# A Trainium2 decoder layer: a thirteenth sevenfold pair in the first half's down passes, four more weight sums made ahead, and the closing scalings cut into 512 and 256 columns

## The chip, the cores and the metric

The kernel runs on one core of one Trainium2 chip. The metric is the device time of one execution in microseconds, taken as the median of several runs of the same program.

## What is computed

One decoder layer over 256 tokens of width 2048 in float32: a normalised input goes through one wide projection, a recurrent branch and a windowed attention branch run side by side, both are gated, merged and projected by `w_out`, and a squared-ReLU MLP of width 8192 follows. The change touches the MLP's down projection, and its preparation is spread over the rest of the layer:

```
x = x + rmsnorm(mix @ w_out, norm_mix_post)
h = rmsnorm(x, norm_mlp_pre)
u = square(relu(h @ w_mlp_up))          # 256 x 8192
x = x + rmsnorm(u @ w_mlp_down, norm_mlp_post)
```

## The kernel before

**Matmuls in two parts.** Every weight chunk and every activation is split into a high part that TensorE takes exactly and a low part, the rest. A product is three matmuls: high by high, high by low, low by high. So each weight half (a tile of 128 by 1024) needs one cast on ScalarE (`whi`, L176) and one subtraction on VectorE (`wlo`, L181). `Stream` (L62) does this for all weights in one order: SyncE loads halves into raw buffers (`wraw`, `xraw`, `more`), the two engines split them into six `whi` and six `wlo` buffers, TensorE uses them. A load waits until the subtraction has read the raw buffer that it goes into; a cast waits until TensorE is done with the `whi` buffer that it goes into.

**The order of the stages.** Projections and attention come first, then the recurrent branch with `attn_proj` (L943 to L959, m = 0 to 3), the merge, the product with `w_out` in two passes (`o_pass`, L1024, called at L1058 and L1076), and the MLP. The MLP runs in two halves f of 4096 channels. Each half makes its 16 activation pairs (the up products, `a_pair`), and then runs two down passes (`down`, L1275), n = 0 and 1, of 1024 output columns each, over the same 16 pairs.

**Sevenfold pairs.** Most of the 16 pairs of a down pass are multiplied by a Strassen-Winograd scheme: seven block products in place of eight, each of three matmuls of 512 columns, so 21 matmuls in place of 24. `KINDS` (L41) gives each pair of each pass a digit. "1" is a plain pair (24 matmuls, two weight halves). The others are sevenfold; they need sums of weight blocks, and the digit says where these are made. With "3" the stream itself makes three of them on VectorE (L149 to L151) just before use. With "2" two blocks come ready from memory and one difference is made in the stream (L147). With "4" everything comes ready. A "1" or "3" loads 1 MB, a "2" 1.25 MB, a "4" 1.75 MB. A sevenfold pair splits three halves and a further 128 by 512 tile (`t2hi`, `t2lo`).

**Sums ahead.** What "2" and "4" read is made earlier by `sums_ahead` (L405), one generator for each such chunk: GpSimd's queue loads the 1 MB chunk into the tile `early` (L410), VectorE adds in place (L414, L416 for a "4" only, L419, L420), and GpSimd's queue writes 0.5 or 1 MB to memory (L422). `in_turn(n, every, wait)` starts n of them, one for each `every` halves of weights that the stream hands out, after `wait` halves. A generator takes one step for each half handed out (`begin`, L204): the load at its first step, L414 and L416 at its fifth, L419 and L420 at its sixth, the write at its seventh. Two rules place them:

```
not_before(nc.gpsimd.dma_start(w, chunks[c]))     # L410: waits for the latest wlo made so far
with tc.issue_after(ws.latest_low.ins):           # L413: VectorE does it after the latest wlo
```

So in the usual course four `wlo` lie between a load and the first sum that reads it.

**The end of the `w_out` product.** In the second pass the last four weight halves are held back (`held`, L1076): the stream hands them out one right behind the other, with no matmul between. TensorE then finishes the first 128 tokens (`last_step`, L1080), then the others. Meanwhile VectorE multiplies the results by a gain (`gained`, L1054), sums the squares, and scales (`norm`, L1089; `scaled`, L1087); TensorE transposes the scaled rows (`turned`, L1103) for the MLP. All of these are pinned in program order on their engines.

**The end of the kernel.** In the last down pass, `finish` (L1448) scales a token block's 2048 outputs and adds the residual with one instruction of 1024 columns and two of 512 (L1484), each followed by a store (L1485).

Of the kernel before, what the change touches and what calls it, by code (L numbers as in the profile page):

```python
# [18 lines left out]
F32 = mybir.dt.float32  # L19
F32R = mybir.dt.float32r  # L20
# [5 lines left out]
P = 128  # L26
# [11 lines left out]

PAIRS = 16

KINDS = ("1242423142424211", "1242423142422411"), ("4242424242421111", "4242424242441111")  # L41
SEVENS = [[p for p in range(PAIRS) if k[0][p] != "1"] for k in KINDS]


# [197 lines left out]
def layer(tc, x, few, kx_first, kx_rest, pos_row, gains, w_q, w_xy, w_rg, w_g, w_rp, w_ap, w_out,  # L242
          w_up, w_dn, out):
    nc = tc.nc
# [35 lines left out]
    for f in range(2):  # L280
        chunks += [w_up[32 * f + i] for i in range(32)]
        for n in range(2):
            sums.update((len(chunks) + i, KINDS[f][n][i]) for i in SEVENS[f])
            plain_down.update(len(chunks) + i for i in range(PAIRS) if i not in SEVENS[f])
            chunks += [w_dn[(2 * f + n) * PAIRS + i] for i in range(PAIRS)]

    def unit(name, dt=F32R):
        return big.tile([P, 4, 2, S], dt, tag="U8", name=name)

    def flat(t):  # L290
        return t.rearrange("p a b c -> p (a b c)")

    ws = Stream(nc, wpool, chunks, sums)

    def units(name):
        return [unit(f"{name}{i}") for i in range(4)]
# [128 lines left out]
    def in_turn(n, every, wait=0):  # L425

        for i in range(wait):
            yield
        left, active, at = [sums_ahead(to_sum.pop(0)) for i in range(min(n, len(to_sum)))], [], 0
        while left or active:  # L430
            if left and at % every == 0:
                active.append(left.pop(0))
            at += 1
            active = [g for g in active if next(g, active) is not active]
            yield
# [11 lines left out]
    def quarter(q):  # L447
        return slice(q * 512, q * 512 + 512)
# [49 lines left out]
    pin = ws.pin = tc.keep_in_program_order  # L498
# [303 lines left out]
    def wide(t):  # L802
        return t.rearrange("p (f t) -> p f t", f=2)
# [126 lines left out]
    def recur(m):  # L930
        room = flat(unit("xct", F32)).rearrange("p (n c) -> p n c", c=512)
        for i in range(2):
            conv(2 * m + i, room[:, i, :])
        for i in range(2):
            gelu(2 * m + i, room[:, 2 + i, :])
# [7 lines left out]
    for m in range(4):  # L943
        if m == 2:
            more = flat(unit("more", F32))
            for i in range(2):
                ws.add(ws.raws, more[:, i * 1024 : i * 1024 + 1024])
        recur(m)
        if m == 0:
            pump(99)  # L950
            ctx_ps.close()
            psg = ctx1.enter_context(tc.tile_pool(name="psg", bufs=2, space=bass.MemoryType.PSUM))
            pairs.append(ctx1.enter_context(tc.tile_pool(name="psa2", bufs=1, space=bass.MemoryType.PSUM)))
        if m < 2:
            ws.side.append(in_turn(2, 6))
            for i in range(2):
                attn_proj(2 * m + i)
        if m < 3:
            gates(m)  # L959
# [50 lines left out]
    x1 = po.tile([P, TB, D], F32, name="x1")  # L1010
# [33 lines left out]

    r1 = []
    late = []
    ws.side.append(in_turn(4, 6, 2))
    h2T = units("h2T")

    def square(tb, q, b):  # L1050
# [135 lines left out]
    for tb in range(TB):  # L1186
        for i in range(2):
            q = 2 + i
# [50 lines left out]

    o_v = out.rearrange("(t p) d -> t p d", p=P)  # L1240

    def evacuate(f, p, u, dst):
        nc.scalar.activation(u, u, AF.Relu)
        nc.scalar.activation(u, u, AF.Square, scale=SHRINK)
        if p not in SEVENS[f]:
            nc.scalar.copy(dst[:, :, 0, :], wide(u))
            nc.vector.tensor_tensor(dst[:, :, 1, :], wide(u), dst[:, :, 0, :].bitcast(F32), ALU.subtract)
            return

        e = u2("e")  # L1250
        u4, e4 = [t.rearrange("p (a b) -> p a b", a=4) for t in (u, e)]
        nc.vector.tensor_tensor(e4[:, 0:2], u[:, 0:P].unsqueeze(1).to_broadcast([P, 2, P]), u4[:, 1:3], ALU.subtract)
        nc.vector.tensor_tensor(e4[:, 2], e4[:, 1], u4[:, 1], ALU.subtract)
        nc.vector.tensor_tensor(e4[:, 3], e4[:, 2], u4[:, 3], ALU.add)
        for to, of in zip(dst, (u4[:, 1:4], e4)):
            nc.scalar.copy(to[:, 0], of)
            nc.vector.tensor_tensor(to[:, 1], of, to[:, 0].bitcast(F32), ALU.subtract)
# [98 lines left out]
    for f in range(2):  # L1356
        uT = {}
        rooms = []
        if f:
            ws.side.append(in_turn(10, 5))  # L1360
        full = []
        for p in range(PAIRS):
            u = u2("u")
            if f == 0 and p == 1:
                ws.side.append(in_turn(7, 4, 8))
            if f == 0 and p in (4, 6):
                not_before(nc.gpsimd.dma_start(h2T_away[p // 2 - 2], h2T[p // 2].bitcast(F32)))
            if f == 0 and p < 2:
                up_pair(p, wide(u))
            else:  # L1370
                a_pair(h2T, wide(u), PRIO if p == PAIRS - 1 else 0)
            full.append((p, u))
            if f == 0 and p == R2_AT:
                pump(99)
                ctx3.close()
                pc = ctx2.enter_context(tc.tile_pool(name="pc", bufs=1))
                ws.small = pc
                ws.add(ws.raws, pc.tile([P, 1024], F32, name="xraw"))
                ws.t2_raws, ws.t2_highs, ws.t2_lows = [[Slot() for i in range(n)] for n in (3, 2, 2)]
            if f == 1 or p >= R2_AT:  # L1380
                for q, u in full:
                    if q % 2 == 0:
                        rooms.append(unit(f"uT{f}{q}"))
                    room = rooms[-1][:, 2 * (q % 2) : 2 * (q % 2) + 2]
                    if q in SEVENS[f]:
                        three = pc.tile([P, 2, 3, P], F32R, tag="three", bufs=max(map(len, SEVENS)), name=f"three{f}{q}")
                        uT[q] = three, flat(room).rearrange("p (a b c) -> p a b c", a=2, b=4)
                    else:
                        uT[q] = room
                    evacuate(f, q, u, uT[q])  # L1390
                full.clear()
# [21 lines left out]
        accs, x1 = [], []  # L1413

        def acc(tb, q):
            return accs[q // 2][:, tb, quarter(q % 2)]
# [31 lines left out]
        def finish(name, b, t, at, w, fold=lambda: None):  # L1448
            tb, i = name
            q = 2 * n + i  # L1450
            a = acc(tb, q)
            if n == 0:
                nc.vector.tensor_tensor(a, b, t, ALU.add)
                nc.scalar.activation(t, a, AF.Square, scale=r2_squared[tb], accum_out=sq3[:, tb, q : q + 1])
                return
            p = slice(at, at + w)
            k = q + (at > 0)
            pin(nc.vector.tensor_tensor(a[:, p], b[:, 0:w], t[:, p], ALU.add))
            if not spare:
                spare.append(flat(unit("spare", F32)))  # L1460
            pin(nc.scalar.activation(spare[0][:, p], a[:, p], AF.Square, scale=r2_squared[tb],
                                     accum_out=sq3[:, tb, k : k + 1]))
            pin(nc.vector.scalar_tensor_tensor(t[:, p], a[:, p], r2_squared[tb],
                                               g3[0][:, q * 512 + at : q * 512 + at + w], ALU.mult, ALU.mult))
            last[tb, i] = t
            fold()
            r, to = [st[:, 12 + 2 * tb + k : 13 + 2 * tb + k] for k in range(2)]
            if at + w < 512:
                pin(nc.vector.tensor_reduce(r, sq3[:, tb, 0:4], AX.X, ALU.add))
                pin(nc.vector.tensor_scalar(before, r, 1.0 / D, EPS, ALU.mult, ALU.add))  # L1470
                return
            if i:
                if tb:
                    pin(nc.scalar.activation(to, sq3[:, tb, 4:5], AF.Sqrt, bias=before, scale=1.0 / D))
                else:
                    pin(nc.vector.tensor_reduce(r, sq3[:, tb, 0:4], AX.X, ALU.add))
                    pin(nc.scalar.activation(to, r, AF.Sqrt, bias=eps, scale=1.0 / D))
                pin(nc.vector.reciprocal(r, to))
                scaled[tb] = r
            if i:  # L1480
                for k in (0, 2, 3):
                    c = quarter(k) if k else slice(0, 1024)
                    g = last[tb, k - 2] if k else accs[0][:, tb]
                    pin(nc.vector.scalar_tensor_tensor(x1[tb][:, c], g, scaled[tb], x1[tb][:, c], ALU.mult, ALU.add))  # L1484
                    pin((nc.scalar if k == 2 else nc.sync).dma_start(o_v[tb][:, c], x1[tb][:, c]))  # L1485

        n = 0
        g3, spare, before = [], [], st[:, 29:30]
# [2 lines left out]
        last, scaled = {}, {}  # L1491
# [82 lines left out]
```

## Time and profile before

| | |
|---|---|
| median of 3 runs | 1481.5 us (1481.31 to 1482.2) |
| the profiled execution | 1481.78 us |
| its span, first to last instruction | 1479.9 us |
| TensorE busy / VectorE / ScalarE | 99% / 80% / 60% |
| mean granted TensorE clock | 0.999 |
| sums ahead (1 MB loads by GpSimd's queue) | 46 |
| moved by DMA | 411 MB, 278 GB/s over the span |

The span is 1.9 us shorter than the profiled execution's own time. PE is TensorE, DVE is VectorE, ACT is ScalarE, POOL is GpSimd, SP is SyncE. Matmuls are pipelined: each lasts 389 ns, but they start closer together than that, so the distance between starts counts. Times in views are from the span's start.

### The profile page before, as it was taken

To read this page: it belongs to the slowest core of one execution; us is meant where nothing else is said; L and a number is where in the kernel's file an instruction comes from. 1 tells how busy PE (TensorE), PEld (TensorE's weight loads), DVE (VectorE), ACT (ScalarE), POOL (GpSimd) and SP (SyncE) were. 2 spreads that over 40 slices of the span, in tenths; PEclk is the share of its full clock that TensorE was granted. 3 is DMA by queue.
4 is the path that set the end of the run, shared out by engine and by line. 5 is a ranking of instruction groups with operands and counts; after the bars stand their busy time and mean duration, and the time that the engine had idled before them with its cause. 6 is when DMAs were issued, how large, how long until landed. Compare 5 with 4: busy or idle time off the path is not lost.

```text
span 1479.9 us, 20692 instructions
## 1 busy us (share of the span) xinstructions
PE 1470.3 (99%) x7520; PEld 1247.2 (84%) x7520; DVE 1182.8 (80%) x1546; ACT 884.4 (60%) x1256; POOL 56.6 (4%) x111
## 2 busy tenths in 40 slices
PE   9999999999999999999999999999999999999997
PEld 8887788888889888888889888888888888888886
DVE  6797888769678957666678788689897877779897
ACT  8564565647566766444345756667574655667673
POOL 0000100000000000000000010000000000000000
PEclk9999999999999999999999999999999999999999
DMA  9878875575757556997795999668898889779794
GB/s 342 282 279 309 316 284 188 194 273 172 277 191 244 177 194 230 314 336 260 295 332 202 314 404 365 195 223 300 306 338 325 295 326 327 284 262 372 240 375 170
DMA packets 114071, 411.09 MB, mean 278 GB/s; under 512 B 12720, under 2 KB 12976, under 8 KB 103856
## 3 DMA queue, kind: packets, MB, share of 16 engines
q1 hardware_dynamic: 98352, 318.53, 61.2%
q0 software_dynamic: 14176, 88.61, 16.2%
q10 hardware_dynamic: 1440, 2.62, 0.5%
q8 instruction: 59, 0.97, 0.3%
q14 instruction: 44, 0.36, 0.1%
HBM read 365.14 MB, written 44.56 MB: 277 GB/s over the span
## 4 chain that ended last, share of the span: by engine, by line
PE 95%; DVE 3%; DMA 2%; ACT 1%; issue 0%; DVEq 0%; ACTq 0%
PE ps L332 22%; PE ps L330 11%; PE s L1262 9%; PE dQ L1262 7%; PE g L370 4%; PE g L372 4%; PE pp L370 4%; PE g L374 4%; PE pp L372 4%; PE pp L374 4%; PE dP L1262 4%; PE q L370 2%; PE q L374 2%; PE q L372 2%; PE kv L532 1%; PE dCs L1262 1%
## 5 line engine op out<-in xcount | busy, mean ns | idle before, releaser
L181 DVE TENSOR_TENSOR wlo<-wraw,whi 128x1024 fp32r<-128x1024 f32 x427 | 517.4, 1220 | 180.8 <-ACT whi L176 177.3
L176 ACT CAST whi<-wraw 128x1024 fp32r<-128x1024 f32 x423 | 442.4, 1050 | 365.4 <-PE pp L374 83.8
L332 PE MATMUL ps<-h2T,whi 128*128 128x512 f32 x704 | 170.8, 390 | 0.1
L332 PEld LDWEIGHTS ps<-h2T,whi 128*128 128x128 f32 x704 | 130.2, 188 | 26.0 <-DVE u L1211 0.3
L332 PE MATMUL ps<-hT,whi 128*128 128x512 f32 x512 | 120.6, 391 | 0.0
L332 PEld LDWEIGHTS ps<-hT,whi 128*128 128x128 f32 x512 | 94.7, 188 | 19.5 <-issue 0.7
L370 PE MATMUL g<-whi,hT 128*128 128x512 f32 x256 | 101.0, 395 | 0.0
L374 PE MATMUL g<-whi,hT 128*128 128x512 f32 x256 | 99.7, 389 | 0.0
L372 PE MATMUL g<-wlo,hT 128*128 128x512 f32 x256 | 99.7, 389 | 0.0
L330 PE MATMUL ps<-h2T,wlo 128*128 128x256 f32 x704 | 91.8, 283 | 0.0
L181 DVE TENSOR_TENSOR wlo<-more,whi 128x1024 fp32r<-128x1024 f32 x72 | 86.2, 1218 | 6.9 <-ACT whi L176 5.8
L330 PEld LDWEIGHTS ps<-h2T,wlo 128*128 128x128 f32 x704 | 89.6, 191 | 2.3
L176 ACT CAST whi<-more 128x1024 fp32r<-128x1024 f32 x72 | 74.8, 1052 | 24.5 <-DVE more L147 4.3
L1262 PE MATMUL dQ<-whi,uT 128*128 128x512 f32 (+1 forms) x198 | 72.2, 384 | 0.0
L330 PEld LDWEIGHTS ps<-hT,wlo 128*128 128x128 f32 x512 | 63.7, 191 | 2.1 <-issue 0.8
L330 PE MATMUL ps<-hT,wlo 128*128 128x256 f32 x512 | 64.6, 283 | 0.0
L181 DVE TENSOR_TENSOR wlo<-xraw,whi 128x1024 fp32r<-128x1024 f32 x44 | 53.6, 1219 | 9.8 <-ACT whi L176 9.8
L176 ACT CAST whi<-xraw 128x1024 fp32r<-128x1024 f32 x44 | 46.2, 1050 | 23.9 <-PE ps L332 10.4
L1262 PE MATMUL s<-whi,uT 128*128 128x512 f32 (+1 forms) x174 | 59.1, 383 | 0.0
L370 PEld LDWEIGHTS g<-whi,hT 128*128 128x128 f32 x256 | 48.1, 188 | 10.6 <-issue 1.0
L374 PEld LDWEIGHTS g<-whi,hT 128*128 128x128 f32 x256 | 48.0, 188 | 10.2
L372 PEld LDWEIGHTS g<-wlo,hT 128*128 128x128 f32 x256 | 48.1, 188 | 9.4
(345 smaller groups left out, 3024.3 us busy)
## 6 DMA issues: line engine op xcount, KB each, us to landing
wraw<-in_w_up SPq DMA_DIRECT2D x104, 512.0 KB, 6.1
early<-in_w_dn POOLq DMA_DIRECT2D x46, 1024.0 KB, 8.6
wraw<-in_w_g SPq DMA_DIRECT2D x58, 512.0 KB, 6.7
wraw<-in_w_xy SPq DMA_DIRECT2D x56, 512.0 KB, 4.4
away<-early POOLq DMA_DIRECT2D x23, 1024.0 KB, 6.6
wraw<-in_w_dn SPq DMA_DIRECT2D x42, 512.0 KB, 6.0
wraw<-in_w_q SPq DMA_DIRECT2D x32, 512.0 KB, 5.4
wraw<-in_w_ap SPq DMA_DIRECT2D x32, 512.0 KB, 4.6
```

Source lines behind the costliest of these rows:

```text
L176: self.pin(self.nc.scalar.copy(hi, src))
L181: self.latest_low = self.pin(self.nc.vector.tensor_tensor(lo, src, hi.bitcast(F32), ALU.subtract))
L330: mm(ps[:, f, 1, :], w, a[:, 0, :], start=False, stop=j == 1 and k == 7)
L332: mm(ps[:, f].rearrange("p a b -> p (a b)"), w, a.rearrange("p a b -> p (a b)"), start=kt == 0, stop=j == 3 and k == 7)
L370: mm(banks[tb][n], a[:, 0, t], hi[:, n * 512 : n * 512 + 512], start=first, stop=False)
L372: mm(banks[tb][n], a[:, 0, t], lo[:, n * 512 : n * 512 + 512], start=False, stop=False)
L374: mm(banks[tb][n], a[:, 1, t], hi[:, n * 512 : n * 512 + 512], start=False, stop=last)
L532: pin(mm(kv[tb], hT[kt // 4][:, kt % 4, x, tb * P : tb * P + P], w[:, c], start=kt == 0 and w is hi and x == 0, stop=kt == KT - 1 and w is ...
L1262: mm(b, a[x], w[y], start=not begun and i == 0, stop=tail and i == 2, skip_group_check=shared)
```

## The change

- `KINDS` of the first half: both passes become "1442424242424211", that is one plain pair, thirteen sevenfold ones (seven "4" and six "2") and two plain ones. Before, each pass had twelve sevenfold pairs (five "4", six "2", one "3") and four plain ones. The second half stays.
- The thirteenth sevenfold pair needs another buffer for its activations (`three13`). It takes the place of the raw buffer `xraw`, which is removed from the ring while the first half's last activations are made, and put back when the second half begins (`fifth`). So the first half's down passes have six raw buffers in place of seven.
- Four more chunks are summed ahead, 50 in place of 46: three in place of two beside `attn_proj` for m = 0 and 1, and six, one each five halves, in place of four, one each six, from the first `w_out` pass on.
- The closing scalings are 512 columns each, and for the last token block the last 512 are two of 256; the order becomes the third quarter, the first, the second, the fourth. Stores alternate between the queues of SP and ACT.

```
-KINDS = ("1242423142424211", "1242423142422411"), ("4242424242421111", "4242424242441111")
+KINDS = ("1442424242424211", "1442424242424211"), ("4242424242421111", "4242424242441111")
...
         if m < 2:
-            ws.side.append(in_turn(2, 6))
+            ws.side.append(in_turn(3, 6))
...
-    ws.side.append(in_turn(4, 6, 2))
+    ws.side.append(in_turn(6, 5, 2))
...
+    def fifth(spent=False):
+
+        if spent:
+            ws.raws.remove(ws.added[0][1])
+            del ws.added[0]
+            return pc.tile([P, 1024], F32R, tag="fifth", bufs=1, name="three13")[:, 0:768].rearrange(
+                "p (a b c) -> p a b c", a=2, b=3)
+        ws.added.insert(0, (ws.raws, Slot(room=pc.tile([P, 1024], F32, tag="fifth", bufs=1, name="xraw"))))
+        ws.raws.insert(0, ws.added[0][1])
...
+        if f:
+            fifth()
...
-                ws.add(ws.raws, pc.tile([P, 1024], F32, name="xraw"))
+                fifth()
...
-                        three = pc.tile([P, 2, 3, P], F32R, tag="three", bufs=max(map(len, SEVENS)), name=f"three{f}{q}")
+                        if SEVENS[f][12:] == [q]:
+                            three = fifth(True)
+                        else:
+                            three = pc.tile([P, 2, 3, P], F32R, tag="three", bufs=12, name=f"three{f}{q}")
...
-                for k in (0, 2, 3):
-                    c = quarter(k) if k else slice(0, 1024)
-                    g = last[tb, k - 2] if k else accs[0][:, tb]
+                for k, a, w in ((2, 0, 512), (0, 0, 512), (1, 0, 512)) + (((3, 0, 256), (3, 256, 256)) if tb else ((3, 0, 512),)):
+                    c, p = slice(k * 512 + a, k * 512 + a + w), slice(a, a + w)
+                    g = acc(tb, k)[:, p] if k < 2 else last[tb, k - 2][:, p]
                     pin(nc.vector.scalar_tensor_tensor(x1[tb][:, c], g, scaled[tb], x1[tb][:, c], ALU.mult, ALU.add))
-                    pin((nc.scalar if k == 2 else nc.sync).dma_start(o_v[tb][:, c], x1[tb][:, c]))
+                    pin((nc.scalar if (k + (a > 0)) % 2 else nc.sync).dma_start(o_v[tb][:, c], x1[tb][:, c]))
```

The table `KINDS` and the calls of `in_turn` set where sums stand on VectorE and on GpSimd's queue. First VectorE at the end of the second `w_out` pass, before the change; `h20` are the rows that `gained` and `scaled` make, and a tile's last number tells the order in which the program made it:

```order
L414 TENSOR_TENSOR early_6797<-early_6797 128x512
L416 TENSOR_TENSOR early_6797<-early_6797 128x512
L181 TENSOR_TENSOR wlo269_6874<-wraw269_6803,whi269_6873 128x1024
L419 TENSOR_TENSOR early_6797<-early_6797 128x512
L420 TENSOR_TENSOR early_6797<-early_6797 128x512
L181 TENSOR_TENSOR wlo270_6894<-wraw270_6821,whi270_6893 128x1024
L181 TENSOR_TENSOR wlo271_6913<-wraw271_6839,whi271_6912 128x1024
L181 TENSOR_TENSOR wlo272_6931<-wraw272_6857,whi272_6930 128x1024
L181 TENSOR_TENSOR wlo273_6949<-wraw273_6877,whi273_6948 128x1024
L1054 TENSOR_TENSOR h20_6377<-o100_6717,gpg2_6374 128x512
L1054 TENSOR_TENSOR h20_6377<-o101_6718,gpg2_6374 128x512
L1092 TENSOR_REDUCE st_177<-sqs_179 128x1
```

The fourth and last sum is over four `wlo` before the first `gained`. The same place after the change:

```order
L414 TENSOR_TENSOR early_6858<-early_6858 128x512
L181 TENSOR_TENSOR wlo271_6935<-wraw271_6864,whi271_6934 128x1024
L419 TENSOR_TENSOR early_6858<-early_6858 128x512
L420 TENSOR_TENSOR early_6858<-early_6858 128x512
L181 TENSOR_TENSOR wlo272_6957<-wraw272_6883,whi272_6956 128x1024
L181 TENSOR_TENSOR wlo273_6978<-wraw273_6901,whi273_6977 128x1024
L414 TENSOR_TENSOR early_6954<-early_6954 128x512
L416 TENSOR_TENSOR early_6954<-early_6954 128x512
L1054 TENSOR_TENSOR h20_6396<-o100_6736,gpg2_6393 128x512
L419 TENSOR_TENSOR early_6954<-early_6954 128x512
L420 TENSOR_TENSOR early_6954<-early_6954 128x512
L1054 TENSOR_TENSOR h20_6396<-o101_6737,gpg2_6393 128x512
```

The sixth sum (`early_6954`) now stands around both `gained`. It was made behind `wlo271_6935` and ahead of `wlo272_6957`, so its load waits for `wlo271`, and two `wlo` lie between the load and L414. GpSimd's queue from the first `w_out` pass on, after the change:

```order
L410 DMA early_6644<-in_w_dn 128x2048
L422 DMA away234_97<-early_6543 128x2048
L410 DMA early_6761<-in_w_dn 128x2048
L422 DMA away235_98<-early_6644 128x1024
L410 DMA early_6858<-in_w_dn 128x2048
L422 DMA away236_99<-early_6761 128x2048
L410 DMA early_6954<-in_w_dn 128x2048
L422 DMA away237_100<-early_6858 128x1024
L422 DMA away238_101<-early_6954 128x2048
```

The sixth load stands behind the fourth sum's write and ahead of the fifth's; two loads and two writes are new on this queue in this stage. TensorE's order is the same up to the first half's down passes.

## Rows read from the trace of the kernel before

**Rows 1.** The page: the span, and each engine's busy time and share.

```profile
span 1479.9 us, 20692 instructions
...
PE 1470.3 (99%) x7520; PEld 1247.2 (84%) x7520; DVE 1182.8 (80%) x1546; ACT 884.4 (60%) x1256; POOL 56.6 (4%) x111
```

**Rows 2.** Windows: stretch, length, busy us per engine (instructions), PEclk, DMA share, GB/s.

```profile
978.00:1057.00 79.00, 79.00 (x350) 65.41 (x349) 72.55 (x74) 53.01 (x61) 1.63 (x3) 1.00 0.86 299
1057.00:1136.00 79.00, 79.00 (x350) 65.42 (x349) 71.73 (x73) 51.70 (x59) 2.18 (x4) 1.00 0.92 330
...
740.00:794.00 54.00, 53.88 (x240) 44.22 (x239) 39.48 (x48) 25.93 (x37) 2.69 (x5) 1.00 0.88 322
```

**Rows 3.** Timeline, TensorE in a down pass: start, us, engine, line, operation, count.

```profile
988.33 0.84 PE L1262 MATMUL s<-more,three 128*128 128x512 f32 x3
989.01 0.84 PE L1262 MATMUL dQ<-more,uT 128*128 128x512 f32 x3
```

**Rows 4.** Timeline, VectorE at the end of the second `w_out` pass.

```profile
765.23 1.21 DVE L181 TENSOR_TENSOR wlo<-wraw,whi 128x1024 fp32r<-128x1024 f32 x1
...
777.52 0.68 DVE L414 TENSOR_TENSOR early<-early 128x512 f32<-128x512 f32 x1
778.24 0.69 DVE L416 TENSOR_TENSOR early<-early 128x512 f32<-128x512 f32 x1
...
781.50 3.50 DVE L181 TENSOR_TENSOR wlo<-wraw,whi 128x1024 fp32r<-128x1024 f32 x3
...
791.16 0.69 DVE L1054 TENSOR_TENSOR h<-o,gpg 128x512 f32<-128x512 f32 x1 [2.03 <-ACT j L1051]
791.77 0.15 DVE L1092 TENSOR_REDUCE st<-sqs 128x1 f32<-128x4 f32 x1
...
792.48 2.74 DVE L1087 SCALAR_TENSOR_TENSOR h<-h,st,xg 128x512 f32<-128x512 f32 x4
```

**Rows 5.** Timeline, TensorE: the first transposes behind the `w_out` product.

```profile
793.65 1.04 PE L1103 MATMUL ptr<-ident,h 128*128 128x128 f32 x8
```

**Rows 6.** Timeline, GpSimd: the last load of a sum in that stage.

```profile
766.85 0.53 POOL L410 DMA_DIRECT2D early<-in_w_dn  x1 [14.24 <-DVE wlo L181]
```

**Rows 7.** Line L410, the loads of all 46 sums: time from issue to landing.

```profile
L410 POOL DMA_DIRECT2D early<-in_w_dn x46: 530/535/682, 58.9 to 1264.4; - x46
...
DMA to landing us min/median/max: 6.3/8.6/12.8
```

**Rows 8.** Windows at the end of the second `w_out` pass.

```profile
775.00:780.00 5.00, 5.00 (x23) 4.14 (x23) 3.49 (x4) 2.73 (x3) 0.00 (x0) 1.00 0.99 388
...
785.00:790.00 5.00, 5.00 (x23) 4.13 (x22) 1.92 (x2) 1.74 (x3) 0.00 (x0) 1.00 0.96 342
```

**Rows 9.** Groups by line, VectorE, 978 to 1136 us: count, busy, mean ns, idle before.

```profile
L181 DVE TENSOR_TENSOR wlo<-wraw,whi 128x1024 fp32r<-128x1024 f32 x38 | 45.7, 1219 | 4.6 <-ACT whi L176 4.0
...
L181 DVE TENSOR_TENSOR t2lo<-t,t2hi 128x512 fp32r<-128x512 f32 x24 | 16.5, 686 | 1.3 <-ACT t2hi L176 1.3
...
L149 DVE TENSOR_TENSOR xraw<-wraw,wraw 128x1024 f32<-128x1024 f32 x1 | 1.2, 1217 | 0.0
```

**Rows 10.** Waits, 978 to 1136 us: waiter, releaser, total us, times, longest.

```profile
ACT t2hi L176 <- PE s L1262: 11.8, 12, 1.0
```

**Rows 11.** The page, DMA issues: count, KB each, median us to landing.

```profile
wraw<-in_w_dn SPq DMA_DIRECT2D x42, 512.0 KB, 6.0
```

**Rows 12.** Timeline, VectorE: the last token block's scalings.

```profile
1473.51 1.29 DVE L1484 SCALAR_TENSOR_TENSOR x<-acc,st,x 128x1024 f32<-128x1024 f32 x1
1474.71 1.41 DVE L1484 SCALAR_TENSOR_TENSOR x<-t,st,x 128x512 f32<-128x512 f32 x2
```

**Rows 13.** Line L1485, the six closing stores: time from issue to landing.

```profile
DMA to landing us min/median/max: 2.7/2.7/2.8
```

**Rows 14.** Windows at the kernel's end.

```profile
1471.90:1476.00 4.10, 0.00 (x0) 0.00 (x0) 3.56 (x6) 0.89 (x3) 0.00 (x0) 1.00 0.09 38
1476.00:1476.50 0.50, 0.00 (x0) 0.00 (x0) 0.12 (x1) 0.00 (x0) 0.00 (x0) 0.93 1.00 393
```

## The prediction

> **What bounds the kernel now.** I read four views, in this order. The page comes first: TensorE is busy 99% of the span, VectorE 80%, ScalarE 60% [rows 1]. The reader should see that a cheaper instruction on any other engine is worth nothing by itself. Then the windows of the two stages that the change touches: in both first-half down passes TensorE is busy in all 79.00 us, and from 740 to 794, around the second `w_out` pass, only 0.12 us is idle [rows 2]. So the time can change in three ways alone: fewer matmuls, a stall of TensorE that is new, or a shorter tail behind its last matmul. The third view is the timeline, to find what the moved instructions would stand in front of; the fourth is the grouped lines and waits, to price them. The sum is made against the profiled execution, 1481.78 us. It lies 0.28 above the median of 1481.5, inside the scatter of the three runs (1481.31 to 1482.2), so I take nothing off for that. A measurement of this kernel can tell about 0.2%, or 3.0 us, from no change: below 1478.5 is faster, above 1484.5 slower.
>
> **Fewer matmuls: -1.36.** One plain pair becomes sevenfold in each of the two passes, 21 matmuls for 24, so six fewer in all. Where three stand in a row in such a pass, the next group starts 989.01 - 988.33 = 0.68 us later [rows 3]. Nothing hides TensorE here, so both passes together give 2 x 0.68 = 1.36.
>
> **What feeds those pairs: nothing.** A "4" in place of a "1" adds one `wlo` and one `t2lo` on VectorE, 1.22 + 0.69 = 1.91 us; a "4" in place of the "3" removes a sum of 1.22 and two of half its size, some 0.69 each, 2.60 [rows 9]. A pass loses 0.7 us of VectorE's 72, which TensorE's 79 cover. If the cover went, a pass would be as long as VectorE's work, still under 73. The loads grow by 2 x 0.75 = 1.5 MB a pass, some 20 GB/s on 299 and 330; the rings have carried 388 [rows 2, 8]. That leaves the sixth raw buffer, which I take up under the rivals.
>
> **Four more sums: nothing, but for one place.** Four sums are four loads of 1 MB, writes, and up to four additions of 0.7 us on VectorE each, spread over three stages. In the `w_out` stage VectorE is busy 39.48 of 54 us [rows 2], and two more sums there need at most 2 x 2.9 = 5.8 of the 14.5 left. On GpSimd's queue a DMA takes 0.53 us to issue [rows 6]. If that cover were gone, TensorE would wait one addition, 0.7 us, for a `wlo` behind it.
>
> **The place: the sixth sum of the `w_out` stage, +4.8.** The second fence of VectorE's order shows it between the last `wlo` and both `gained`, and its load is made to wait for `wlo271`.
> - When the load starts. `wlo271` is the second of the three that take 3.50 us from 781.50 [rows 4], so it ends at 781.50 + 2 x 1.17 = 783.8. The last load of this kind started at 766.85, when the `wlo` it waits for had ended at 765.23 + 1.21 = 766.44 [rows 4, 6], 0.4 later. I take 784.3. Ahead of it on GpSimd's queue is only the fourth sum's write, which is due before.
> - When it lands. 46 such loads took 6.3, 8.6 and 12.8 us (least, median, most) [rows 7], so the data is there at 790.6, 792.9 or 797.1. I take the median. The rings were 0.96 to 0.99 busy around this time [rows 8], which speaks against the least.
> - What waits behind it. VectorE works in order. L414 holds L416, the first `gained`, L419, L420, the second `gained` and the sum of squares. In the kernel before, the second `gained` ran at 791.16 and the reduction at 791.77 [rows 4]; before the change four `wlo` stood here, and now only two do, since the stream hands out the held halves one behind the other and the generator counts halves, not time.
> - From L414 to the reduction there are four additions 0.72 apart (778.24 - 777.52) and two `gained` 0.61 apart, 2.88 + 1.22 = 4.1. So the reduction is at 797.0. Behind it the first scaled rows end 792.48 + 0.75 - 791.77 = 1.46 later, of which 0.75 is a quarter of the 2.74 with its overhead [rows 4]: at 798.5.
> - What TensorE needs. It starts the transposes of these rows at 793.65 [rows 5], with nothing else in its pinned order to do. It stalls 798.5 - 793.65 = 4.8 us. With the other landings the stall is 2.5 or 9.0.
>
> With a load of 3.8 us it would land at 788.1 and cost nothing; the shortest of 46 took 6.3. The stall is not given back later, since TensorE has no idle time there to shrink.
>
> **The closing: -0.4.** Before, a scaling of 1024 columns (the next starts 1.20 later) and two of 512 ended at 1474.71 + 1.41 = 1476.12 [rows 12]. Now three of 512 and two of 256 follow each other. By the spacing of those 512s, about 0.66, and some 0.41 for a 256 (an estimate: half of the 512's own part and a like start), the last ends at about 1476.4, 0.28 later. Against that the first store leaves about 0.5 earlier, and the last store carries half the bytes; stores take 2.7 us from issue to landing, and behind 1476 the rings carry 393 GB/s [rows 13, 14], so some of their 1 MB is moved earlier. From below: all of the 0.65 us that 0.25 MB takes at 393 GB/s is won. From above: nothing of it is won but a start of two small ones, +0.25. I take -0.4, nearer to the row of the rings, since they are full there.
>
> **The sum.** 1481.78 - 1.36 - 0.4 + 4.8 = 1484.8, or 3.3 above the median, 0.22%. With the bounds of the stall alone it runs from 1482.5 to 1489.0.
>
> **Rival 1: the wait is short or is not there, 1480.0.** If the data has landed by 788.1, what is left is -1.36 - 0.4: 1481.78 - 1.76 = 1480.0. For it: rings that are less busy than before at this moment, since SP's loads of the up projection wait for buffers. Against it: none of the 46 loads took under 6.3 [rows 7]. The Trainium skill, in "DMA: Bandwidth & Descriptors", section "Anatomy of one DMA — SWDGE (gpsimd) path", prices a DMA at about 2.0 us and its bytes at 436 GB/s. By that price, an estimate, this 1 MB load would take 4.4 us, land at 788.7 and stall TensorE 0.6, for a time near 1480.6. The loads of rows 7 don't agree with that figure: on rings shared with the weights the least is 1.9 us above it.
>
> **Rival 2: TensorE's clock falls in the stall, 1486.9.** At the kernel's end TensorE had its last matmul by 1471.90; the granted clock stayed at 1.00 up to 1476.0 and was 0.93 in the half microsecond behind that, so part of it was at 1.2 GHz in place of 2.4 [rows 14]. A stall of 4.8 us is of that length. If the clock falls in it, the matmuls behind run at half speed for a time. No row shows how long; an equal span of some 4.2 us at half speed would cost 2.1, for 1484.8 + 2.1 = 1486.9. The Trainium skill, in "TensorE: Matmul & The Clock Gate", section "HAM oscillation — how this bites in real kernels", names a DMA wait between groups of matmuls as what throttles the engine again. The end of this trace agrees that an idle TensorE loses the clock; no row here shows it between matmuls.
>
> **Rival 3: six raw buffers are too few, 1487.8.** In the first half's down passes a raw buffer is now taken away while the loads grow. A buffer is busy from its load's issue until its subtraction: 6.0 us to land [rows 11] and about 3.1 for the cast, the subtraction and their turn. A "4" sends three halves of 512 KB through the raw buffers in some 4.76 us (21 matmuls at 0.68 / 3), so six buffers give each a cycle of 6 x 4.76 / 3 = 9.5. So a landing of up to 6.4 us is hidden, and each microsecond over that costs TensorE about half a microsecond a pair, once the halves in stock are used. For it: the median is close to the point, and the rings get busier (0.86 and 0.92 now [rows 2]). Against it: ScalarE waited there for TensorE to release buffers, 11.8 us in 12 waits [rows 10], so data was early, not late. At 0.3 us a pair over some ten pairs I price it at 3: 1484.8 + 3.0 = 1487.8.
>
> **Chances and range.** The forecast with its stall of 2.5 to 9 us has 0.47, the missing wait 0.22, the clock 0.18, the buffers 0.10, and 0.03 is for a gain that I don't see. The forecast's own range is 1482.5 to 1489.0. From 1479.5 (rival 1 with the larger closing gain) to 1488.5 leaves out the top of the stall's range and the worst of rivals 2 and 3. No case that I can name gains 3.0 us, so faster has the 0.03. Slower than 1484.5 are rivals 2 and 3 and a little over half of the forecast, 0.54; the rest, 0.43, is within the bound.
>
> **What would show it.** The profile after should count 7514 matmuls, and both first-half down passes should still be full on TensorE, each 0.7 us shorter; idle time there that ends with a raw load is rival 3. Near 787 to 793 VectorE's last L414 of the `w_out` stage should stand idle behind the DMA of `early`, and TensorE should be idle behind 793.65 until the first scaled rows. If TensorE has no gap there, rival 1 holds; a granted clock under 1.00 in the first microseconds behind the gap is rival 2. The tail shows its part by the distance from the last matmul to the last store. I am wrong if that gap is under 2.5 us, or if TensorE has a gap of over 1 us anywhere else.

## The result, and the profile after

The changed kernel takes 1494.21 us, the median of five runs (1492.96 to 1496.32); the kernel before took 1481.82 beside it (1481.31 to 1482.38). The ratio is 1.0085, with an interval of 1.0074 to 1.0097: slower by 12.4 us, or 0.8%. The profiled execution of the change took 1495.33 us; its span is 13.6 us longer than that of [rows 1].

The page of the changed kernel, span and busy times:

```profile
span 1493.5 us, 20775 instructions
...
PE 1475.6 (99%) x7514; PEld 1250.2 (84%) x7514; DVE 1191.6 (80%) x1567; ACT 887.9 (59%) x1261; POOL 60.8 (4%) x119
```

TensorE has its six matmuls fewer, and still is busy 5.3 us longer than in [rows 1]. Matmuls that take longer are the first sign of the clock. What TensorE waited for, in the whole execution (waiter, releaser, total us, times, longest):

```profile
PE ptr L1103 <- DVE h L1087: 4.7, 1, 4.7
PE o L1083 <- ACT whi L176: 2.9, 1, 2.9
PE warm L496 <- DVE ones L480: 1.1, 1, 1.1
PE o L1083 <- DVE wlo L181: 0.8, 1, 0.8
```

The wait at L496 belongs to the start. The other three are new, 8.4 us together, and all lie in the `w_out` product and the norm behind it. The windows there (columns as in [rows 2]):

```profile
740.00:785.00 45.00, 44.89 (x199) 36.84 (x198) 33.11 (x39) 19.38 (x25) 3.20 (x6) 1.00 0.87 306
785.00:790.00 5.00, 2.42 (x11) 1.69 (x9) 0.69 (x1) 0.77 (x1) 0.00 (x0) 1.00 1.01 418
790.00:795.00 5.00, 3.91 (x9) 2.95 (x10) 4.65 (x5) 2.96 (x5) 1.07 (x2) 0.60 0.73 251
795.00:800.00 5.00, 5.00 (x17) 3.96 (x17) 0.13 (x1) 0.69 (x2) 0.00 (x0) 0.72 0.93 299
800.00:805.00 5.00, 1.38 (x7) 0.80 (x5) 3.94 (x7) 0.28 (x2) 0.54 (x1) 0.96 0.42 171
805.00:810.00 5.00, 3.94 (x14) 3.46 (x15) 4.34 (x8) 3.50 (x8) 0.00 (x0) 0.50 0.51 210
810.00:815.00 5.00, 5.00 (x34) 4.66 (x33) 3.45 (x7) 2.85 (x7) 0.00 (x0) 0.85 0.31 105
```

Read PE's busy time and PEclk together. Two holes in the busy time (785 to 795, 800 to 810), and behind each a granted clock of 0.50 to 0.85, between the two levels of 1.2 and 2.4 GHz. Busy time times what the clock lacks is 3.91 x 0.40 + 5.00 x 0.28 + 1.38 x 0.04 + 3.94 x 0.50 + 5.00 x 0.15 = 5.7 us. The busy time of the page gives a little more: 5.3 us longer, with 1.4 us of matmuls fewer, is 6.7 us of slower matmuls. So 8.4 of waiting and some 6 to 7 of lost clock, less the gain of the matmuls, make up the difference.

**The second hole** is the forecast one. VectorE's timeline around it answers to [rows 4]:

```profile
786.34 0.69 DVE L414 TENSOR_TENSOR early<-early 128x512 f32<-128x512 f32 x1 [2.10 <-DMA early<-in_w_dn]
790.31 1.23 DVE L181 TENSOR_TENSOR wlo<-wraw,whi 128x1024 fp32r<-128x1024 f32 x1 [3.28 <-ACT whi L176]
...
800.68 0.69 DVE L414 TENSOR_TENSOR early<-early 128x512 f32<-128x512 f32 x1 [5.55 <-DMA early<-in_w_dn]
...
804.54 0.14 DVE L1092 TENSOR_REDUCE st<-sqs 128x1 f32<-128x4 f32 x1
```

Ahead of the sixth sum's L414 VectorE stands idle for 5.55 us, until the DMA lands; the reduction comes 3.9 behind it, and TensorE's transposes, which answer to [rows 5], wait for the rows scaled after that:

```profile
806.05 1.97 PE L1103 MATMUL ptr<-ident,h 128*128 128x128 f32 x8 [4.67 <-DVE h L1087]
```

Their eight take 1.97 us in place of 1.04: that is the clock again.

**The first hole** was not forecast. TensorE's timeline at the held weight halves, and ScalarE's cast that it waits for:

```profile
790.33 0.51 PE L1083 MATMUL o<-whi,mixT 128*128 128x512 f32 x1 [2.91 <-ACT whi L176]
791.59 0.80 PE L1083 MATMUL o<-wlo,mixT 128*128 128x512 f32 x1 [0.76 <-DVE wlo L181]
```

```profile
789.23 1.04 ACT L176 CAST whi<-wraw 128x1024 fp32r<-128x1024 f32 x1 [6.25 <-DMA wraw<-in_w_out]
```

The cast waits for the last of the held halves to land. GpSimd's queue, which answers to [rows 6], shows what went out just before that half was asked for:

```profile
765.13 0.53 POOL L410 DMA_DIRECT2D early<-in_w_dn  x1 [12.91 <-DVE wlo L181]
767.47 0.54 POOL L422 DMA_DIRECT2D away<-early  x1 [1.81 <-DVE early L420]
777.15 0.53 POOL L410 DMA_DIRECT2D early<-in_w_dn  x1 [9.14 <-DVE wlo L181]
778.48 0.54 POOL L422 DMA_DIRECT2D away<-early  x1 [0.80 <-DVE early L420]
791.94 0.53 POOL L410 DMA_DIRECT2D early<-in_w_dn  x1 [12.93 <-DVE wlo L181]
```

In the kernel before no load of a sum followed the one at 766.85 [rows 6] in this stage. Here the fifth sum's 1 MB and the fourth's write went out at 777.15 and 778.48. The half behind them, line L117 from 779.1 to 779.4:

```profile
L117 SPq DMA_DIRECT2D wraw<-in_w_out x1: 328/328/328, 779.2 to 779.2; - x1
...
DMA to landing us min/median/max: 9.9/9.9/9.9
```

The same line of the kernel before, from 772.2 to 772.5:

```profile
L117 SPq DMA_DIRECT2D wraw<-in_w_out x1: 328/328/328, 772.3 to 772.3; - x1
...
DMA to landing us min/median/max: 8.3/8.3/8.3
```

So the half is asked for 6.9 us later, since its raw buffer came free later, and then takes 1.6 longer.

Those 6.9 us are older than the fifth sum: its load went out only 2.1 us ahead of the half's. They begin with a half asked for at 750.0, 1.4 us behind the third sum's load; it took 9.4 us to land. ScalarE's cast waited for it:

```profile
759.44 1.05 ACT L176 CAST whi<-wraw 128x1024 fp32r<-128x1024 f32 x1 [3.42 <-DMA wraw<-in_w_out]
```

On VectorE a `gained` waited for what ScalarE does behind that cast, and the next `wlo` stands behind the `gained`:

```profile
761.11 0.69 DVE L1054 TENSOR_TENSOR h<-o,gpg 128x512 f32<-128x512 f32 x1 [2.59 <-ACT j L1051]
...
763.51 1.22 DVE L181 TENSOR_TENSOR wlo<-wraw,whi 128x1024 fp32r<-128x1024 f32 x1
```

SyncE's next load waited for this `wlo` and went out at 764.8, 2.9 us later than the same load before (761.9); until then the rings ran nearly empty. The same two microseconds before and after:

```profile
764.00:766.00 2.00, 2.00 (x11) 1.65 (x10) 2.00 (x3) 0.87 (x1) 0.00 (x0) 1.00 0.91 240
```

```profile
764.00:766.00 2.00, 2.00 (x11) 1.65 (x10) 2.00 (x3) 1.00 (x1) 0.53 (x1) 1.00 0.08 12
```

So the loss does not come of rings that are fuller over the whole stretch. From 740 to 785 they were 0.87 busy in the changed kernel (the first window above), and in the one before:

```profile
740.00:785.00 45.00, 44.88 (x198) 36.79 (x197) 35.12 (x40) 21.61 (x27) 2.69 (x5) 1.00 0.91 331
```

**What held.** The down passes of the first half, from their first matmul to the first of the next stage. Before:

```profile
978.13 0.39 PE L1262 MATMUL dQ<-whi,uT 128*128 128x512 f32 x1
...
1135.89 0.62 PE L332 MATMUL ps<-h2T,whi 128*128 128x512 f32 x2
```

After:

```profile
993.07 0.39 PE L1272 MATMUL dQ<-whi,uT 128*128 128x512 f32 x1
...
1149.47 0.62 PE L332 MATMUL ps<-h2T,whi 128*128 128x512 f32 x2
```

That is 157.76 us before and 156.40 after: 1.36 less, as forecast. The windows over these two passes answer to [rows 2]; TensorE is full in both:

```profile
991.90:1070.90 79.00, 79.00 (x350) 65.42 (x350) 71.90 (x73) 55.32 (x64) 1.64 (x3) 1.00 0.91 322
1070.90:1149.40 78.50, 78.50 (x348) 65.03 (x347) 72.11 (x73) 53.84 (x60) 2.18 (x4) 1.00 0.95 337
```

At the end, the last two scalings answer to [rows 12] and the closing stores to [rows 13]:

```profile
1489.09 0.88 DVE L1499 SCALAR_TENSOR_TENSOR x<-t,st,x 128x256 f32<-128x256 f32 x2
```

```profile
DMA to landing us min/median/max: 2.0/2.2/3.4
```

TensorE's last matmul, before and here:

```profile
1471.58 0.28 PE L1262 MATMUL s<-whi,uT 128*128 128x256 f32 x1
```

```profile
1485.16 0.28 PE L1272 MATMUL s<-whi,uT 128*128 128x256 f32 x1
```

Here it starts 8.3 us ahead of the span's end at 1493.5; before, with the span's end at 1479.9, 8.3 as well. The closing part gained nothing.

### The profile page after: what moved, and what is told of

Its sections match the earlier page's. It is cut to its first block, busy times and chain, and to the rows that moved or that the text cites. A ratio compares the mean times of both kernels' runs of the same rounds, so it can differ in the third digit from the quotient of the medians.

```text
span 1493.5 us, 20775 instructions
## 1 busy us (share of the span) xinstructions
PE 1475.6 (99%) x7514; PEld 1250.2 (84%) x7514; DVE 1191.6 (80%) x1567; ACT 887.9 (59%) x1261; POOL 60.8 (4%) x119
## 4 chain that ended last, share of the span: by engine, by line
PE 90%; DMA 4%; DVE 3%; issue 1%; ACT 1%; DVEq 0%; POOL 0%; ACTq 0%; POOLq 0%
PE ps L332 21%; PE ps L330 11%; PE s L1272 9%; PE dQ L1272 7%; PE g L370 4%; PE g L374 4%; PE pp L374 4%; PE g L372 4%; PE pp L372 4%; PE pp L370 4%; PE dP L1272 4%; DMA wraw<-in_w_out 3%; PE q L370 2%; PE q L374 2%; PE q L372 2%; PE kv L532 2%
## 5 line engine op out<-in xcount | busy, mean ns | idle before, releaser
L176 ACT CAST whi<-wraw 128x1024 fp32r<-128x1024 f32 x438 | 456.7, 1050 | 375.8 <-PE pp L374 83.1
L181 DVE TENSOR_TENSOR wlo<-wraw,whi 128x1024 fp32r<-128x1024 f32 x442 | 534.1, 1219 | 182.7 <-ACT whi L176 181.3
L1272 PE MATMUL dQ<-whi,uT 128*128 128x512 f32 (+1 forms) x184 | 66.7, 383 | 0.0
L414 DVE TENSOR_TENSOR early<-early 128x512 f32<-128x512 f32 x50 | 34.3, 686 | 27.2 <-DMA early<-in_w_dn 27.2
L410 POOL DMA_DIRECT2D early<-in_w_dn x50 | 26.9, 537 | 617.5 <-DVE wlo L181 404.8
```

What stands on the lines that cost most here:

```text
L176: self.pin(self.nc.scalar.copy(hi, src))
L181: self.latest_low = self.pin(self.nc.vector.tensor_tensor(lo, src, hi.bitcast(F32), ALU.subtract))
L414: v.tensor_tensor(t1, t1, t3, ALU.add)
L1272: mm(b, a[x], w[y], start=not begun and i == 0, stop=tail and i == 2, skip_group_check=shared)
```

## The experiments

Theory A: the whole loss arises in the `w_out` stage, out of two causes, the late last half and the wait at the norm, each with its own loss of clock. Its rivals: the sums' bytes alone are behind both holes (B, and D in another form), or the first half's down passes pay too (C). The twelve runs are compared with the kernel before on the same chip (medians 1482.1, 1481.68 and 1482.1 for the three groups of four).

### First group: undo the sums' places, one by one

Neither of the two sums in the `w_out` stage (all edits are made in the changed kernel unless said otherwise):

```
-            ws.side.append(in_turn(3, 6))
+            ws.side.append(in_turn(4, 6))
...
-    ws.side.append(in_turn(6, 5, 2))
+    ws.side.append(in_turn(4, 6, 2))
```

> The change, but with the w_out stage's sums as before (four, one each six halves) and the two others moved beside attn_proj (four each for m = 0 and 1). Theory A (all of the loss arises in the w_out stage, from the two added sums): no stall of TensorE from 740 to 815, clock 1.00 there, and what is left is the gain of six matmuls, 1.4, with a tail worth 0 to 0.4: 1480.0 to 1480.5. Theory B (only the fifth sum's bytes matter) gives the same here. Theory C (the first half's down passes pay, with six raw buffers or the 1.5 MB more): 1484 or more, with idle TensorE in those passes.

1482.83 us, ratio 1.0007 (0.9998 to 1.0015): the loss is gone, but not all of the gain came, and the time is above the range given. TensorE had no wait behind 750 us; it had this one, early in the kernel:

```profile
PE pg L894 <- ACT room L900: 0.9, 1, 0.9
```

It is at 428 us, in the gates behind `attn_proj`, and neither kernel has it. The place that I had given the moved sums has a price of its own.

Five sums, with `in_turn(5, 5, 2)` in the `w_out` stage and `in_turn(4 - m, 6)` beside `attn_proj`:

> The change with five sums in the w_out stage, one each five halves; the sixth is moved beside attn_proj m = 0. The fifth sum stays where its load and the fourth one's write go out just ahead of the last held weight half. Theory A: the wait at the transposes is gone, the late last half stays, 3 to 4 us of stall and about 3 more at the lower clock: 1486 to 1488. Theory B: the same stall, and the time is nearly that of the whole change, 1492 to 1494. Theory C: 1484 or more with no idle time from 740 to 815.

1487.58 us, ratio 1.0041 (1.0029 to 1.0054), inside the range for another reason: 2.6 us of wait at the same gates, and only 1.8 at the held halves, with the clock at 1.00. A run without the gates' wait was needed.

Four sums as before, and one that starts where the sixth did:

```
-            ws.side.append(in_turn(3, 6))
+            ws.side.append(in_turn(4 - m, 6))
...
-    ws.side.append(in_turn(6, 5, 2))
+    ws.side.append(in_turn(4, 6, 2))
+    ws.side.append(in_turn(1, 5, 27))
```

> The change with four sums as before in the w_out stage, one each six halves, and a fifth that starts at the half at which the change starts its sixth; so the rings are less crowded before the held halves, and one sum still stands around both gained rows. Theory A: no late weight half, a stall of 3 to 6 us at the transposes, about 3 more at the lower clock: 1486 to 1489. Theory B (the sum there is late only because the rings are crowded): a stall under 1 us, 1480 to 1481.5. Theory C: 1484 or more with no idle time from 740 to 815.

1495.16 us, ratio 1.0096 (1.0081 to 1.0112). No half is late, and the transposes wait 7.8 us, more than A had said; the gates near 428 us wait another 1.4. The time is far above A's range of 1486 to 1489. B falls, since the wait at the norm comes without a late half ahead of it.

The sums' places alone, in the kernel before (its `KINDS`, raw buffers and closing):

```
-            ws.side.append(in_turn(2, 6))
+            ws.side.append(in_turn(3, 6))
...
-    ws.side.append(in_turn(4, 6, 2))
+    ws.side.append(in_turn(6, 5, 2))
```

> The kernel before with only the calls of in_turn of the change (three and three beside attn_proj, six each five halves in the w_out stage); KINDS, buffers and tail as before, so the last stage has four sums fewer. Theory A: both stalls and both clock losses as in the change, without its six matmuls fewer: 1494 to 1497. Theory B: the same. Theory C: 1481 to 1483.

1496.78 us, ratio 1.0104 (1.009 to 1.0117). The two lines that place the sums make the whole loss without anything else of the change; C falls. This trace has 5.2 us of wait at the held halves and 7.0 at the transposes, and none at the gates.

### Second group: what holds TensorE, and where the sums can go

The sixth sum's load stays, its additions and its write come six halves later (`later` is 6 for the last sum of that stage, 0 elsewhere):

```
-        for i in range(4):
+        for i in range(4 + later):
             yield
```

> The change with one thing moved: the sixth sum's additions and write come six weight halves later (its load stays where it is, and so do all six loads). Theory A (VectorE, held by the sixth load, is what TensorE waits for at the transposes): that stall and the clock lost behind it go, 4.7 + 2.6 us in the changed kernel's trace, and the late last half stays with 2.9 + 0.8 and some 3.6 of clock: 1486 to 1488. Rival D (the sixth load's bytes on the rings hold up what the norm needs): the transposes still wait 3 us or more, 1491 to 1495.

1487.62 us, ratio 1.0043 (1.0029 to 1.0058). The wait at the transposes is gone with the same load on the rings, so D falls: VectorE, held by the load, was what TensorE waited for. The late half stays (1.9 and 0.6 us), and the up stage has a wait of 2.8 for VectorE that no expectation had. The six runs of this kernel scatter widely, from 1484.38 to 1493.02, so its time says less than its waits.

The six sums one each four halves, `in_turn(6, 4, 2)`:

> The change with the six sums of the w_out stage one each four halves in place of five, so the last one's additions stand ahead of the last two held halves and not at the norm; the bytes of the stage are the same, but earlier. Theory A: no wait at the transposes; rings fuller ahead of the held halves, so a late half of 1 to 5 us with 0 to 3.5 of clock: 1482 to 1489. Rival D: as the whole change, 1491 to 1495.

1486.98 us, ratio 1.0036 (1.0024 to 1.0048). No wait at the transposes; the held halves are late twice, 2.2 us for `whi` and 1.2 for `wlo`. The same six sums, closer together, still make the end of the stage late.

Four sums in the `w_out` stage, three and three beside `attn_proj`, and the two others in the second half's up stage (`in_turn(12, 5)` for `in_turn(10, 5)`):

> The change with the w_out stage's sums as before (four, one each six halves) and the two others made in the second half's up stage (12 in place of 10, one each five halves), three and three beside attn_proj as in the change. Theory A: no stall from 740 to 815; also none at the gates near 428 us, where four sums beside attn_proj (run of neither) cost 1.5; six matmuls fewer are worth 1.4 and the tail nothing: 1480.0 to 1481.0. Theory C (the sixth raw buffer or the down passes' bytes cost): 1482 or more.

1482.32 us, ratio 1.001 (1.0001 to 1.0018). That is above A's range and in C's. The trace speaks against C, though: the `w_out` stage is whole, the first half's down passes have no wait, and TensorE waits 1.3 us for VectorE (`u`, L360) at 1315 us, in the second half. That place has a price too.

The same with the two sums in the first half's up stage:

```
-    ws.side.append(in_turn(6, 5, 2))
+    ws.side.append(in_turn(4, 6, 2))
...
-                ws.side.append(in_turn(7, 4, 8))
+                ws.side.append(in_turn(9, 4, 8))
```

> The same, but the two sums go to the first half's up stage (nine in place of seven, one each four halves). The rings are busiest there (0.91 from 800 to 900 in the kernel before), so if bytes alone make a weight late, it is here: Theory A without such a cost 1480.0 to 1481.0, with it 1482 to 1486.

1480.58 us, ratio 0.9991 (0.9982 to 0.9999): faster than both kernels, by 1.1 us than the one before. All that TensorE waits for is what it waited for before, and 0.2 us for one `wlo`. The windows show how busy the rings were there:

```profile
800.00:900.00 100.00, 100.00 (x624) 90.51 (x623) 87.21 (x125) 66.60 (x101) 6.40 (x12) 1.00 0.90 336
900.00:976.00 76.00, 76.00 (x441) 67.43 (x440) 59.23 (x80) 45.26 (x62) 4.26 (x8) 1.00 0.81 284
```

The two sums run behind 900 us, where the rings are 0.81 busy with them and were 0.70 busy in the kernel before. That this is why the place is free was not tried.

### Third group: each cause alone, on the best version

Five sums one each five halves, `in_turn(5, 5, 2)`, and eight in the up stage:

> The version with two sums moved to the first half's up stage, changed in one thing: five sums in the w_out stage, one each five halves, and eight in the up stage. It is the fifth sum alone, without the stall at the gates that the earlier run of it had. Theory A: the last held half is late by 1.8 us as there, or by up to the 3.7 of the whole change; 1482.4 to 1486.

1488.50 us, ratio 1.004 (1.0027 to 1.0052); above the range given. TensorE's waits:

```profile
PE o L1083 <- ACT whi L176: 3.2, 1, 3.2
...
PE o L1083 <- DVE wlo L181: 0.8, 1, 0.8
```

The late half is 4.0 us by itself, and the windows behind it show the clock:

```profile
790.00:795.00 5.00, 3.24 (x8) 2.35 (x9) 3.99 (x5) 3.73 (x5) 0.54 (x1) 0.64 0.52 202
795.00:800.00 5.00, 5.00 (x17) 3.97 (x16) 2.14 (x4) 0.69 (x2) 0.00 (x0) 0.67 0.97 302
```

3.24 x 0.36 + 5.00 x 0.33 = 2.8 us more. The spacing of five in place of six is part of this run; it wasn't tried apart from the fifth sum. In the first run with five sums the last half landed in 8.1 us, here in 11.1, and there the stall was 1.8.

The same with the fifth sum's additions left out, its load and its write kept:

```
         with tc.issue_after(ws.latest_low.ins):
-            v.tensor_tensor(t2, t2, t1, ALU.add)
-            v.tensor_tensor(t4, t4, t2, ALU.add)
+            if adds:
+                v.tensor_tensor(t2, t2, t1, ALU.add)
+                v.tensor_tensor(t4, t4, t2, ALU.add)
```

(`adds` is false for the last sum of that stage; L414 and L416 likewise.)

> The run before it with the fifth sum's additions left out: its chunk is loaded and written back as it is, so the bytes on the rings are the same and the products of one chunk are not those of the reference. Theory A1 (the bytes make the last half late): the same stall and time as with the additions, within 0.5 us. Theory A2 (the additions hold the wlo, and with it the raw buffers): no stall, 1480.2 to 1481.0.

1487.79 us, ratio 1.0036 (1.0023 to 1.005), with waits of 3.7 and 0.8. The time is 0.7 us off the run with the additions, a little more than the 0.5 allowed, while each of the two scatters by over 4 us. The half is as late without the fifth sum's additions as with them, so A2 falls. What is left of A1 is the transfers, but not those of the fifth sum alone: its load went out at 776.87, and the half was asked for 2.1 us later, when most of the delay was there already. The earlier sums, one each five halves, keep their transfers and additions in this run. How much the spacing does and how much the fifth sum stays open, since four sums one each five halves were not run. The half's own load, line L117 from 778.8 to 779.1:

```profile
L117 SPq DMA_DIRECT2D wraw<-in_w_out x1: 328/328/328, 779.0 to 779.0; - x1
...
DMA to landing us min/median/max: 11.0/11.0/11.0
```

Four sums as before in the `w_out` stage and a fifth that starts at the sixth's place, `in_turn(1, 5, 27)` as above, and eight in the up stage:

> The version with two sums moved to the up stage, with four sums in the w_out stage as before and a fifth that starts at the half of the change's sixth, and eight in the up stage. It is the wait at the norm alone. Theory A: 5 to 8 us of stall at the transposes and 2 to 3.5 more at the lower clock, and no late half: 1488 to 1492.

1488.24 us, ratio 1.0042 (1.0029 to 1.0054). One wait, at the transposes:

```profile
PE ptr L1104 <- DVE h L1088: 5.2, 1, 5.2
```

Behind it stands 5.00 us of work at a clock of 0.50, 2.5 us:

```profile
800.00:805.00 5.00, 5.00 (x20) 4.31 (x19) 4.35 (x7) 2.02 (x3) 0.00 (x0) 0.50 0.03 11
```

The best version with the closing scalings and stores of the kernel before:

> The version with two sums moved to the up stage, with the closing scalings and stores of the kernel before. If the closing of the change is worth the 0.4 us of the prediction: 1481.0. By the traces, where the span ends 8.05 us behind the last matmul before and 8.06 after the change: nothing, 1480.6.

1480.66 us, ratio 0.9991 (0.9982 to 0.9999), against 1480.58 with the same ratio, each to the kernel before on its own chip: the closing is worth nothing that these runs can see.

Over this run the late half alone costs 7.8 us and the wait at the norm alone 7.6, 15.4 together, where the whole change lies 13.6 above the best version. The two do not quite add up; no run says why.

## Why the prediction was wrong

The direction was right, slower, and the size was not: 3.3 us over the median was forecast, and 12.4 came, above the range. The sign of being wrong that the prediction names came too: a second gap of over 1 us, the 2.9 at the held halves.

**The six matmuls, -1.36: right.** The trace shows 1.36, and the best version is 1.1 faster than before.

**The wait at the norm, +4.8: right, by the mechanism given.** The change waits 4.7, and alone it is 5.2; L414 stood idle behind the DMA as foretold. The times of the steps all moved by some 7.6 us, because the first hole came ahead of them: the load was issued at 791.94 and not at 784.3, and TensorE was ready for the transposes later by as much. It landed in 8.7 us, where the median taken from [rows 7] was 8.6. That 4.7 came so near to 4.8 is in part luck: the same wait was 5.2, 7.0 and 7.8 us in other runs, all inside the 2.5 to 9.0 given. The run with this wait alone is the cleaner test: its load went out at 784.84, where 784.3 was forecast.

**The step that failed: "Four more sums: nothing, but for one place".** It priced a sum by VectorE's additions and by the 0.53 us of an issue on GpSimd's queue, and left out what its transfers do to the weights' loads on the same rings. The rings were in view, 0.99 busy from 775 to 780 [rows 8], and I used that figure only for the sixth load's own landing. In its place the runs showed this: a half whose load stood close behind a sum's transfers landed late (9.4 us in place of 6.6 for the one at 750.0, 9.9 in place of 8.3 for the last), a raw buffer that is filled later is free later, and the next load of it starts later. The mean load of the rings does not tell of it: from 740 to 785 they were less busy than before. The cover that I named, slack of VectorE, was not the one that counted. This term is +3.7 in the change and +4.0 alone, with the fifth sum's additions or without them; its division between the fifth sum and the closer spacing is not shown.

**The second step that failed: rival 2's place.** The clock was given a chance of 0.18 and 2.1 us, and as an alternative. It came with both holes and costs some 5.7 together. Alone it is 2.8 behind the late half and 2.5 behind the wait at the norm, but 1.2 in the run without the additions (3.10 x 0.30 + 5.00 x 0.05) and nothing in the first run with five sums. The Trainium skill, in "TensorE: Matmul & The Clock Gate", section "HAM oscillation — how this bites in real kernels", says that a wait for a DMA between groups of matmuls can throttle the engine, so that the next group starts at the lower clock. The trace agrees (0.60, 0.72 and 0.50 in the windows above), already behind a wait of 2.9 us, where the page's example has waits of some 3 to 5. A forecast that puts a stall of some us on TensorE has to carry the clock in its sum.

**The closing, -0.4: wrong, it is 0.** The last scaling ends 1489.09 + 0.88 - 1485.16 = 4.8 us behind the start of the last matmul, where it was 1476.12 - 1471.58 = 4.5; the last stores take 2.2 in place of 2.7. The 0.2 that is left doesn't show in the span.

**Rival 3, six raw buffers: did not come.** Both passes are full, and in the run of the sums alone the loss was there with seven.

With the failed terms put in, 1481.78 - 1.36 + 4.7 + 3.7 + 5.7 = 1494.5, against 1495.33 of the execution that the terms are read from; with the 6.7 of the busy time for the clock it is 1495.5. The median is 1494.21.

## What to carry to other kernels

Price work that is moved "beside" other work on every resource that it takes, and ask which loads its transfers will stand in front of: here five sums one each five halves, in place of four one each six, made TensorE wait 4.0 us for the last weights, and leaving the fifth sum's additions out did not help. Where an engine works in order, ask of each instruction that waits for a DMA what is queued behind it, and place it where nothing urgent is. And when TensorE stalls for some microseconds, add what the clock may take afterwards: here it was some 6 us on 8.4 of waiting.

## What was not expected of the hardware

The clock fell behind stalls shorter than I had reckoned with. After the last matmul of the kernel before it stayed at 1.00 for 4.1 us [rows 14]. In the change it was 0.60 from 790 to 795, behind a wait of 2.9 us; in the run with the additions later, with waits of 1.9 and 0.6 us, the window from 790 to 795 shows 0.50:

```profile
790.00:795.00 5.00, 4.38 (x11) 3.34 (x11) 4.91 (x6) 2.48 (x4) 1.06 (x2) 0.50 0.66 209
```

In the first run with five sums, with waits of 1.0 and 0.8 us, it stayed at 1.00:

```profile
790.00:795.00 5.00, 3.15 (x12) 1.76 (x11) 4.46 (x7) 2.88 (x3) 0.00 (x0) 1.00 0.79 306
```

The second surprise is that two of the three other places for these two sums had a price as well (the gates near 428 us, the second half at 1315 us), and so had the sixth sum's additions when they were moved into the up stage: in a program in which TensorE is almost never idle, a place is free only where a run has shown it.
